# One half-head's loads moved ahead of the finished half-head's last sums, and the softmax maximum formed negated, in a hybrid attention block

## The chip, the cores and the metric

The kernel runs on one core of a Trainium2 chip. The metric is device time in microseconds (us) of the whole kernel, the median of several runs. The engines are TensorE (PE in the profile, its weight loads PEld), VectorE (DVE), ScalarE (ACT), GpSimd (POOL) and SyncE (SP, which issues every DMA of this kernel).

## What is computed

One decoder layer on a sequence of 2048 tokens with 1024 channels, in float32: token mixing, then a SwiGLU feed-forward part, then a norm. The change touches token mixing, which has two attention branches.

- Branch A: twelve heads of 64 channels in three groups. Group g attends with dilation 1, 4 or 16 inside a band of 129 keys, with a linear (ALiBi) bias. The outputs of the three groups are merged with weights from their softmax denominators.
- Branch B: four heads of "forgetting attention", causal over the whole sequence:

```python
s = einsum('bqhd,bkhd->bhqk', qi, k) * scale
s = s + (Fi[..., :, None] - F[..., None, :])
s = where(kpos[None, :] <= qpos[:, None], s, -inf)
out = einsum('bhqk,bkhd->bqhd', softmax(s), v)
```

Each branch goes through an up-projection, is gated and summed, and one output projection follows.

## The kernel before

**Program order and issue order.** The kernel is traced in program order. At build time a planner then lays out one fixed queue of instructions for each engine. It takes instructions as their operands and their tile slots become ready on its own timeline, earlier program order first. So a load may stand in SP's queue far ahead of its place in the program, if a slot for its tile is free. On the chip each queue runs in order, and semaphores hold an instruction until its operands are there.

**Tile slots.** On-chip buffers are slots that tiles of one tag share (`SLOTS`, L77). Three tags matter here. `big` has 11 slots of 8 KB per partition: the queries, keys and key remainders of a branch A head take three, those of a branch B half-head two or four, and each up-projection pass takes four for its tiles `y` (L993). `mid` has 6 slots of 4 KB: branch A's values `va` and the rows `nf` of branch B. `bigx` has 3 slots, for `utok` and the merge tiles `uw`.

**Branch A** (`branch_a`, `head_a`). For each of 12 heads and four quarters u, `scores` makes four blocks of 128 queries by 128 or 256 keys: two matmuls into PSUM (L769, L773), one DVE instruction that adds the bias, writes the logits to SBUF and takes the row maximum (L775), then one small DVE instruction that negates the four maxima (L778), and four exponentials on ACT (L783). `sums` transposes the exponentials on PE, copies them out and multiplies them with the values.

**Branch B** (`branch_b`, `head_f`, `half_tiles`). Heads 0 and 1 are done whole; heads 2 and 3 are done as halves of the queries, in the order

```python
FOX = ((None, 0), (None, 1), (0, 2), (0, 3), (1, 2), (1, 3))
```

where the first number is the half (0: queries 0 to 1023, 1: queries 1024 to 2047) and the second the head. I write half-head (1, 2) for the second half of head 2. `head_f` starts by asking for its data: `half_tiles` issues the loads of queries `qs` (L710), keys `kh` and `kl` (L712) and values `vhl` (L713), and L840 the rows `nf`. `scores(cq, b)` works on 128 queries against all keys up to them, in segments of 512: POOL makes the bias (L854, L859), PE two matmuls (L866), DVE adds, writes logits and carries the maximum from segment to segment (L868); then DVE negates the maximum (L874), ACT takes the exponentials and their sums `dp` (L878), and DVE adds the segments' sums up (L880). `sums(cq)` follows one step later: transposes (L902), a split into two float32r parts (L106, L107), and matmuls with the values (L910), for 256 queries; every second time it writes the result out (L922), and that counts in `f_done`.

**The order around the change.** Two generators run side by side by a clock of costs written by hand, first branch A and B, later the up-projection `up(0)` and B:

```python
together([(ga, PACE[0]), (gb, 1.0)])
merge_weights()
together([(gb, 1.0)], lambda: f_done[0] >= 12)
gu = up(0)
together([(gu, PACE[1]), (gb, 1.0)])
for g in (gb, gu, up(1)): ...
```

Branch A ends while half-head (0, 3) is in its last score passes. `merge_weights` (L973 to L988) works out branch A's merge weights and stores them (`wrow`). B then runs until (0, 3) is written out, which is the twelfth time. Only then is `up(0)` traced, and `half_tiles` for (1, 2) after the first step of `up(0)`. The first four steps of `up(cp)` load branch outputs and weights for half of the tokens (L999, L1005), multiply and add them on DVE (L1007, L1009) and split the result into the `y` tiles; sixteen more steps each multiply with up-projection weights (L100 to L102 into psZ), apply two gates on DVE (L1034), add on POOL (L1035) and store. Ten of the sixteen steps of `up(0)` stand among the score passes of the last two half-heads.

Of the kernel before, what the change touches and what calls it, by code (L numbers as in the profile page):

```python
# [10 lines left out]
F32 = mybir.dt.float32  # L11
# [48 lines left out]
def trunk(ctx, tc, x, c, w_ada, b_ada, norm_mix, w_in, b_forget, w_up_a, w_up_b, w_out,  # L60
# [63 lines left out]
    cst.tile([P, 16], F32, name="fill")  # L124
# [620 lines left out]
    def head_a(h):  # L745
# [5 lines left out]
        mx = sm.tile([P, NT], F32, tag="mxa", name="mxa")  # L751
# [3 lines left out]
        def scores(u):  # L755
# [4 lines left out]
            for b in range(4):  # L760
                if b % 2 == 0:
                    s = psS("A")
                bb = 4 * u + b
                so = s[:, (b % 2) * 256:(b % 2) * 256 + 256]
                k0 = bb * P if first[b] else (bb - 1) * P
                o0 = P if first[b] else 0
                for i, kk in enumerate((kh, kl)):
                    if g == 2:
                        PE.matmul(so[:, o0:].rearrange("p (c n) -> p c n", c=NCH), qs[:, bb * P:(bb + 1) * P],  # L769
                                  kk.rearrange("p (c r n) -> p r c n", c=NCH, r=16)[:, bb],  # L770
                                  start=(i == 0), stop=(i == 1))
                    else:
                        PE.matmul(so[:, o0:], qs[:, bb * P:(bb + 1) * P], kk[:, k0:(bb + 1) * P],  # L773
                                  start=(i == 0), stop=(i == 1))
                V.tensor_tensor_reduce(out=Lb(b, o0, 256), in0=so[:, o0:], in1=bias[:, o0:],  # L775
                                       scale=1.0, scalar=NEG, op0=ALU.add, op1=ALU.max,
                                       accum_out=mx[:, bb:bb + 1])
            V.tensor_scalar(nm[:, 4 * u:4 * u + 4], mx[:, 4 * u:4 * u + 4], -1.0, None,  # L778
                            op0=ALU.mult)
            for b in range(4):  # L780
                bb = 4 * u + b
                o0 = P if first[b] else 0
                A.activation(Lb(b, o0, 256), Lb(b, o0, 256), AF.Exp, bias=nm[:, bb:bb + 1])  # L783
            return Lb, first

        def sums(u, Lb, first):
# [42 lines left out]
            PE.transpose(pst[:NT, :P], mx, ident)  # L829
# [5 lines left out]
    def head_f(h, part):  # L835
# [7 lines left out]
        def scores(cq, b):  # L843
            if cq % 2 == 0 and b == 0:
                den[cq // 2] = sm.tile([P, 4], F32, tag="den", name="den", bufs=4)
            qb = 2 * cq + b
            nk = (qb + 1) * P
            dq = den[cq // 2][:, qb % 4:qb % 4 + 1]
            mx = sm.tile([P, 4], F32, tag="mx", name="mx", bufs=4)
            segs = list(range(0, nk, CH))  # L850
            for i, sg in enumerate(segs):
# [13 lines left out]
                for j, kk in enumerate((kh, kl)):  # L865
# [4 lines left out]
                    scale=1.0, scalar=NEG if i == 0 else mx[:, i - 1:i],  # L870
                    op0=ALU.add, op1=ALU.max, accum_out=mx[:, i:i + 1])
            n = len(segs)
            nm = sm.tile([P, 1], F32, tag="nmf", name="nmf", bufs=4)
            V.tensor_scalar(nm, mx[:, n - 1:n], -1.0, None, op0=ALU.mult)  # L874
            dp = sm.tile([P, 4], F32, tag="dp", name="dp", bufs=4)
            for i, sg in enumerate(segs):
                e = min(sg + CH, nk)
                A.activation(Ls[cq, b, sg][:, :e - sg], Ls[cq, b, sg][:, :e - sg], AF.Exp, bias=nm,  # L878
                             accum_out=dp[:, i:i + 1])
            V.tensor_reduce(out=dq, in_=dp[:, :n], op=ALU.add, axis=mybir.AxisListType.X)  # L880

        def sums(cq):
            if cq % 2:
                dn = den[cq // 2]
# [43 lines left out]
    def branch_b():  # L928
# [3 lines left out]
        for part, h in FOX:  # L932
            scores, sums = head_f(h, part)
# [7 lines left out]
            if (part, h) in (FOX[-1], FOX[-3]):  # L941
                yield from behind()
                behind = None
# [20 lines left out]
    def merge_weights():  # L964
# [9 lines left out]
        for g in (1, 2):  # L974
            V.tensor_tensor(v3(M, g), v3(M, g), tok(g), op=ALU.max)
        for g in range(3):
            V.tensor_tensor(v3(es[g], g), tok(g), v3(M, g), op=ALU.subtract)
# [257 lines left out]
```

## Time and profile before

| | |
|---|---|
| Three runs | 2929.98 us median, 2927.61 to 2929.99 |
| The profiled execution | 2929.82 us, of which 2927.8 us are the span from first to last instruction |
| Busy share of the span | PE 95%, DVE 70%, ACT 47%, POOL 6% |
| Mean granted TensorE clock | 0.983 of full speed |

The busy share is a mean over stages. The attention stage lies between about 840 and 1455 us from the start; before it are the input projections, after it the output projection and the feed-forward part. PE's busy time is modelled, and matmuls are pipelined, so a PE that is 97% busy may still have small gaps.

### The profile page before, as it was taken

Reading aid. Unit: us, or ns where it says so; the run is one execution under the profiler, and the core shown is the slowest. Engines: PE = TensorE matmul, PEld = TensorE weight load, DVE = VectorE, ACT = ScalarE, POOL = GpSimd, SP = SyncE. Lnnn points to the kernel's source line nnn. Section 1 sums busy time; section 2 is a strip of 40 time slices with the busy share of each in tenths; the row PEclk is TensorE's granted clock in tenths of the full one; section 3 lists DMA queues with packets and bytes.
Section 4 is the critical chain, followed back from the end, with each engine's and each line's share of the span. In section 5 each row is a group of like instructions: output and inputs, shape, how many; then the busy total and the mean of one; then the engine's idle time right before and its main releaser. Section 6 shows DMA issues by size and latency. Waiting matters only on the chain.

```text
span 2927.8 us, 40828 instructions
## 1 busy us (share of the span) xinstructions
PE 2776.7 (95%) x13778; PEld 2310.3 (79%) x13778; DVE 2050.0 (70%) x4283; ACT 1376.6 (47%) x2726; POOL 182.2 (6%) x291
## 2 busy tenths in 40 slices
PE   7999999999999999478799999999999999989998
PEld 6789888988888888367577788888888888878876
DVE  5865578576647888676877866656855557796887
ACT  4653345344447778444355633334433335343543
POOL 0000000000002223242300000000000000000000
PEclk9999999999999999789999999999999999999999
DMA  7687476467856767766956654443522235785642
GB/s 245 167 222 216 130 218 196 152 172 204 249 190 229 239 179 205 231 193 197 324 174 211 200 174 144 144 158 116 176 78 85 87 113 161 219 259 178 214 156 99
DMA packets 524089, 534.70 MB, mean 183 GB/s; under 512 B 91716, under 2 KB 374748, under 8 KB 517724
## 3 DMA queue, kind: packets, MB, share of 16 engines
q1 hardware_dynamic: 523880, 532.11, 58.4%
q8 instruction: 108, 1.77, 0.2%
q14 instruction: 101, 0.83, 0.1%
HBM read 360.70 MB, written 171.29 MB: 182 GB/s over the span
## 4 chain that ended last, share of the span: by engine, by line
PE 45%; DVE 2%; DMA 2%; issue 1%; ACT 1%; POOLq 0%; DVEq 0%; SPq 0%; ACTq 0%
PE psX L100 9%; PE psX L101 9%; PE psX L102 8%; PE psZ L100 4%; PE psZ L101 4%; PE psZ L102 4%; PE psY L102 2%; PE psY L100 2%; PE psY L101 2%; DMA pc<-wfg 1%; PE psT L1110 0%; DVE wl L107 0%; DMA out_dram<-x 0%; ACT wh L106 0%; DVE wt L217 0%
## 5 line engine op out<-in xcount | busy, mean ns | idle before, releaser
L106 ACT ACTIVATE wh<-wt 128x512 fp32r<-128x512 f32 (+1 forms) x464 | 288.5, 623 | 628.1 <-PE psX L101 338.6
L107 DVE TENSOR_TENSOR wl<-wt,wh 128x512 fp32r<-128x512 f32 (+1 forms) x464 | 313.6, 679 | 258.8 <-ACT wh L106 241.6
L106 ACT ACTIVATE wh<-wr 128x512 fp32r<-128x512 f32 (+1 forms) x324 | 201.5, 623 | 428.2 <-PE psX L101 233.5
L107 DVE TENSOR_TENSOR wl<-wr,wh 128x512 fp32r<-128x512 f32 (+1 forms) x324 | 219.4, 678 | 201.4 <-ACT wh L106 184.5
L217 DVE TENSOR_TENSOR wt<-wr 128x512 f32<-128x512 f32 (+1 forms) x216 | 147.2, 681 | 11.6 <-DMA wr<-in_w_in_dram 4.8
L217 DVE TENSOR_TENSOR wt<-wr,wt 128x512 f32<-128x512 f32 (+1 forms) x216 | 146.5, 678 | 3.7
L244 ACT ACTIVATE u<-psX 128x512 f32<-128x512 f32 x216 | 125.6, 582 | 8.7 <-PE psX L102 8.7
L854 POOL TENSOR_SCALAR bi<-nf,F_col 128x512 f32<-128x512 f32 (+3 forms) x160 | 107.1, 670 | 303.1 <-DVE mx L868 258.7
L878 ACT ACTIVATE L<-L,nmf 128x512 f32<-128x512 f32 (+3 forms) x160 | 103.1, 647 | 36.0 <-DVE nmf L874 35.9
L106 ACT ACTIVATE ph<-psT 128x512 fp32r<-128x512 f32 (+1 forms) x110 | 61.3, 566 | 71.5 <-PE psT L902 71.0
L1140 DVE TENSOR_TENSOR ac<-psZ,u 128x512 f32<-128x512 f32 x88 | 60.3, 685 | 41.4 <-PE psZ L102 40.2
L107 DVE TENSOR_TENSOR pl<-psT,ph 128x512 fp32r<-128x512 f32 (+1 forms) x110 | 70.5, 646 | 20.6 <-ACT ph L106 20.2
L811 PE MATMUL psY<-pf,va 128*65 128x128 f32 (+1 forms) x408 | 78.8, 327 | 0.8 <-DVE den L880 0.2
L775 DVE CUSTOM_DVE_ANT_0 L<-psX,bias 128x128 f32<-128x128 f32 (+1 forms) x192 | 64.1, 356 | 18.8 <-PE psX L773 14.1
L910 PE MATMUL psY<-pl,vhl 128*128 128x256 f32 x248 | 70.4, 311 | 6.6 <-DVE pl L107 5.7
L910 PE MATMUL psY<-ph,vhl 128*128 128x256 f32 (+1 forms) x248 | 72.0, 302 | 4.4 <-ACT ph L106 3.2
L783 ACT ACTIVATE L<-L,nm 128x128 f32<-128x128 f32 (+1 forms) x192 | 72.2, 450 | 5.5 <-DVE nm L778 4.7
L100 PE MATMUL psZ<-y,wu 128*128 128x512 f32 x128 | 54.4, 425 | 17.9 <-DVE gt L1034 13.9
L100 PE MATMUL psX<-f_A11h,wh 128*128 128x512 f32 x176 | 69.4, 394 | 0.0
L902 PE MATMUL psT<-ident,L 128*128 128x128 f32 x410 | 67.6, 285 | 1.8 <-DVE pl L107 1.8
L101 PE MATMUL psX<-f_A11l,wh 128*128 128x512 f32 x176 | 69.0, 392 | 0.0
L102 PE MATMUL psX<-f_A11h,wl 128*128 128x512 f32 x176 | 69.0, 392 | 0.0
(542 smaller groups left out, 8701.2 us busy)
## 6 DMA issues: line engine op xcount, KB each, us to landing
x<-x SPq DMA_DIRECT2D x192, 256.0 KB
wr<-in_w_ffn_in_dram SPq DMA_DIRECT2D x88, 512.0 KB
wr<-in_w_in_dram SPq DMA_DIRECT2D x64, 512.0 KB
qk<-sh SPq DMA_DIRECT2D x192, 128.0 KB
act<-ac SPq DMA_DIRECT2D x88, 256.0 KB
pc<-wfg SPq DMA_DIRECT2D x77, 256.0 KB
qk<-st SPq DMA_DIRECT2D x128, 128.0 KB
wa<-in_w_ada_dram SPq DMA_DIRECT2D x64, 256.0 KB
```

The source lines that it names most:

```text
L100: PE.matmul(o, lh, rh, start=first, stop=False, skip_group_check=True)
L101: PE.matmul(o, lh, rl, start=False, stop=False, skip_group_check=True)
L102: PE.matmul(o, ll, rh, start=False, stop=last, skip_group_check=True)
L106: A.activation(hi, src, AF.Copy)
L107: V.tensor_tensor(lo, src, raw(hi), op=ALU.subtract)
L217: V.tensor_tensor(v[i], *made[i](g, v), op=ALU.subtract)
L244: A.activation(t, o, AF.Copy, scale=1.0 if scale is None else scale)
L783: A.activation(Lb(b, o0, 256), Lb(b, o0, 256), AF.Exp, bias=nm[:, bb:bb + 1])
L811: PE.matmul(uo[:65, qb_[0] * P:qb_[0] * P + w], va[:, 4 * u + kb_, :], pf[:, pos:pos + w], start=i_ == 0, stop=i_ == len(runs) - 1, skip_g ...
L854: G.tensor_scalar(bi[:, :e - sg], nf[sg // D][:, sg % D:sg % D + e - sg], 1.0, F_col[:, qb * NHB + h:qb * NHB + h + 1], op0=ALU.mult, op1= ...
L878: A.activation(Ls[cq, b, sg][:, :e - sg], Ls[cq, b, sg][:, :e - sg], AF.Exp, bias=nm, accum_out=dp[:, i:i + 1])
L910: f_pe[0] = PE.matmul(uo[:, q0:256], vhl[:, kb, :], p_[:, 256 * i:256 * i + 256 - q0], start=(kp == 0 and i == 0 and j == 0), stop=(last a ...
```

## The change

Three things. First, after the last score pass of (0, 3) the next half-head's `head_f(2, 1)`, with all of its loads, is traced ahead of the last `sums` of (0, 3), of its write-out and of the first step of `up(0)`. The same line does nothing at the end of (1, 3), which is the last. The rest of the program order is as it was. Second, the score instructions of both branches scale by -1 and take a minimum, so that they leave the negated logits and the negated maximum; the two small negating instructions go, and the exponential takes scale -1. The branch A merge reads the negated maxima, with `max` turned into `min` and the two operands of a subtraction swapped. Third, the sums `dp` of four score passes are kept in one tile and added up by one DVE instruction in `sums`, once for 512 queries. A filler tile grows by 16 columns, which belongs to no instruction.

```diff
--- before.py
+++ after.py
@@ -121,7 +121,7 @@
         return r
 
 
-    cst.tile([P, 16], F32, name="fill")
+    cst.tile([P, 32], F32, name="fill")
     ident = cst.tile([P, P], F32, name="ident")
     make_identity(nc, ident)
     ones = cst.tile([P, P], F32, name="ones")
@@ -748,7 +748,6 @@
         qs, kh, kl, va = head_tiles(h // 2, 6 + h // 2, h % 2, g, sl, d)
         bias = slot("pc", "bias", [P, 256])
         G.tensor_scalar(bias, base, float(slopes[h] * d), 0.0, op0=ALU.mult, op1=ALU.add)
-        mx = sm.tile([P, NT], F32, tag="mxa", name="mxa")
         nm = sm.tile([P, NT], F32, tag="nm", name="nm")
         ut = slot("bigx", "utok", [65, T])
 
@@ -773,14 +772,12 @@
                         PE.matmul(so[:, o0:], qs[:, bb * P:(bb + 1) * P], kk[:, k0:(bb + 1) * P],
                                   start=(i == 0), stop=(i == 1))
                 V.tensor_tensor_reduce(out=Lb(b, o0, 256), in0=so[:, o0:], in1=bias[:, o0:],
-                                       scale=1.0, scalar=NEG, op0=ALU.add, op1=ALU.max,
-                                       accum_out=mx[:, bb:bb + 1])
-            V.tensor_scalar(nm[:, 4 * u:4 * u + 4], mx[:, 4 * u:4 * u + 4], -1.0, None,
-                            op0=ALU.mult)
+                                       scale=-1.0, scalar=-NEG, op0=ALU.add, op1=ALU.min,
+                                       accum_out=nm[:, bb:bb + 1])
             for b in range(4):
                 bb = 4 * u + b
                 o0 = P if first[b] else 0
-                A.activation(Lb(b, o0, 256), Lb(b, o0, 256), AF.Exp, bias=nm[:, bb:bb + 1])
+                A.activation(Lb(b, o0, 256), Lb(b, o0, 256), AF.Exp, bias=nm[:, bb:bb + 1], scale=-1.0)
             return Lb, first
 
         def sums(u, Lb, first):
@@ -826,7 +823,7 @@
             SP.dma_start(u_scr[h // 2][(h % 2) * 64:(h % 2) * 64 + 64, :], ut[:64, :])
             SP.dma_start(den_scr[h].rearrange("(a t) -> a t", a=1), ut[64:65, :])
             pst = ps("Y")
-            PE.transpose(pst[:NT, :P], mx, ident)
+            PE.transpose(pst[:NT, :P], nm, ident)
             str_ = slot("pc", "str", [NT, P])
             V.tensor_copy(str_, pst[:NT, :P])
             SP.dma_start(sta_scr[h], str_)
@@ -842,11 +839,12 @@
 
         def scores(cq, b):
             if cq % 2 == 0 and b == 0:
-                den[cq // 2] = sm.tile([P, 4], F32, tag="den", name="den", bufs=4)
+                den[cq // 2] = [sm.tile([P, 4, cq // 2 + 1], F32, tag=f"dp{cq // 2}", name="dp"),
+                                sm.tile([P, 4], F32, tag="den", name="den")]
             qb = 2 * cq + b
             nk = (qb + 1) * P
-            dq = den[cq // 2][:, qb % 4:qb % 4 + 1]
-            mx = sm.tile([P, 4], F32, tag="mx", name="mx", bufs=4)
+            dp = den[cq // 2][0][:, qb % 4, :]
+            nm = sm.tile([P, 4], F32, tag="nmf", name="nmf", bufs=4)
             segs = list(range(0, nk, CH))
             for i, sg in enumerate(segs):
                 e = min(sg + CH, nk)
@@ -867,21 +865,18 @@
                               start=(j == 0), stop=(j == 1))
                 V.tensor_tensor_reduce(
                     out=L[:, :e - sg], in0=s[:, :e - sg], in1=bi[:, :e - sg],
-                    scale=1.0, scalar=NEG if i == 0 else mx[:, i - 1:i],
-                    op0=ALU.add, op1=ALU.max, accum_out=mx[:, i:i + 1])
+                    scale=-1.0, scalar=-NEG if i == 0 else nm[:, i - 1:i],
+                    op0=ALU.add, op1=ALU.min, accum_out=nm[:, i:i + 1])
             n = len(segs)
-            nm = sm.tile([P, 1], F32, tag="nmf", name="nmf", bufs=4)
-            V.tensor_scalar(nm, mx[:, n - 1:n], -1.0, None, op0=ALU.mult)
-            dp = sm.tile([P, 4], F32, tag="dp", name="dp", bufs=4)
             for i, sg in enumerate(segs):
                 e = min(sg + CH, nk)
-                A.activation(Ls[cq, b, sg][:, :e - sg], Ls[cq, b, sg][:, :e - sg], AF.Exp, bias=nm,
-                             accum_out=dp[:, i:i + 1])
-            V.tensor_reduce(out=dq, in_=dp[:, :n], op=ALU.add, axis=mybir.AxisListType.X)
+                A.activation(Ls[cq, b, sg][:, :e - sg], Ls[cq, b, sg][:, :e - sg], AF.Exp,
+                             bias=nm[:, n - 1:n], scale=-1.0, accum_out=dp[:, i:i + 1])
 
         def sums(cq):
             if cq % 2:
-                dn = den[cq // 2]
+                dp, dn = den[cq // 2]
+                V.tensor_reduce(out=dn, in_=dp, op=ALU.add, axis=mybir.AxisListType.X)
                 V.reciprocal(dn, dn)
                 pd = ps("Y")
                 PE.transpose(pd[:4, :P], dn, ident)
@@ -929,8 +924,10 @@
 
 
         behind = None
-        for part, h in FOX:
-            scores, sums = head_f(h, part)
+        nxt = None
+        for at_, (part, h) in enumerate(FOX):
+            scores, sums = nxt or head_f(h, part)
+            nxt = None
             for cq in range(4 if part else 0, 4 if part == 0 else 8):
                 for b in range(2):
                     scores(cq, b)
@@ -939,6 +936,9 @@
                         yield from behind()
                 behind = lambda sums=sums, cq=cq: sums(cq)
             if (part, h) in (FOX[-1], FOX[-3]):
+                if at_ + 1 < len(FOX):
+
+                    nxt = head_f(FOX[at_ + 1][1], FOX[at_ + 1][0])
                 yield from behind()
                 behind = None
     f_end, f_done, f_pe = [None], [0], [None]
@@ -972,9 +972,9 @@
         M, Dn, *es = [mw[:, i, :] for i in range(5)]
         V.tensor_copy(M, md[0][:, 0, 0, :])
         for g in (1, 2):
-            V.tensor_tensor(v3(M, g), v3(M, g), tok(g), op=ALU.max)
+            V.tensor_tensor(v3(M, g), v3(M, g), tok(g), op=ALU.min)
         for g in range(3):
-            V.tensor_tensor(v3(es[g], g), tok(g), v3(M, g), op=ALU.subtract)
+            V.tensor_tensor(v3(es[g], g), v3(M, g), tok(g), op=ALU.subtract)
             A.activation(es[g], es[g], AF.Exp)
         for g in range(3):
             if g == 0:
```

## Rows read from the trace of the kernel before

**Rows 1.** The page: busy time by engine, and PE's busy tenths in 40 slices.

```profile
PE 2776.7 (95%) x13778; PEld 2310.3 (79%) x13778; DVE 2050.0 (70%) x4283; ACT 1376.6 (47%) x2726; POOL 182.2 (6%) x291
...
PE   7999999999999999478799999999999999989998
```

**Rows 2.** Busy time by stretch: stretch, its length, then busy us (and instructions).

```profile
core 0: us, PE busy (x) PEld busy (x) DVE busy (x) ACT busy (x) POOL busy (x), PEclk, DMA share, GB/s
880.00:1187.50 307.50, 293.57 (x2063) 254.18 (x2062) 249.37 (x977) 239.98 (x577) 83.08 (x168) 0.99 0.67 205
960.00:1000.00 40.00, 39.28 (x286) 34.32 (x284) 33.45 (x115) 28.00 (x69) 9.27 (x21) 1.00 0.71 232
1150.00:1160.00 10.00, 9.82 (x82) 9.18 (x81) 8.62 (x45) 9.93 (x29) 3.93 (x8) 1.00 0.10 21
1187.50:1216.50 29.00, 0.28 (x3) 0.14 (x2) 12.67 (x17) 1.53 (x3) 0.00 (x0) 0.58 0.79 226
1206.00:1216.50 10.50, 0.00 (x0) 0.00 (x0) 3.71 (x4) 0.00 (x0) 0.00 (x0) 0.50 1.03 325
1216.50:1376.00 159.50, 130.24 (x682) 106.49 (x683) 119.40 (x271) 79.28 (x190) 61.23 (x80) 0.88 0.68 207
```

**Rows 3.** The timeline of PE around its hole: start, duration, instruction, [idle before].

```profile
1173.76 0.28 PE L769 MATMUL psX<-kl,qs 128*128 128x128 f32 x1
...
1187.50 0.28 PE L910 MATMUL psY<-pl,qv 128*128 128x128 f32 x1
...
1216.52 1.22 PE L866 MATMUL psX<-kh,qs 128*128 128x512 f32 x2 [28.74 <-DMA kh<-qk]
```

**Rows 4.** Waits of PE, 1216 to 1360 us: total, times, longest.

```profile
PE psX L866 <- DMA kh<-qk: 28.7, 1, 28.7
...
PE psX L866 <- DMA kl<-qk: 1.2, 1, 1.2
```

**Rows 5.** The timeline of SP's queue, 1140 to 1280 us.

```profile
1143.39 0.54 SPq L840 DMA_DIRECT2D nf<-nf  x1
...
1180.10 0.32 SPq L832 DMA_DIRECT2D sta<-str  x1
...
1190.37 1.54 SPq L988 DMA_DIRECT2D wrow<-mw  x3
...
1205.94 0.52 SPq L710 DMA_DIRECT2D qs<-qk  x1
1206.55 0.38 SPq L712 DMA_DIRECT2D kh<-qk  x1
```

**Rows 6.** The timeline of ACT: the first write to a `y` tile.

```profile
1204.08 1.15 ACT L106 ACTIVATE y<-uw 128x512 fp32r<-128x512 f32 x2 [15.88 <-DVE uw L1009]
```

**Rows 7.** DMA issues, 1140 to 1280 us: count and KB each.

```profile
kh<-qk SPq DMA_DIRECT2D x2, 1024.0 KB
```

**Rows 8.** DVE by shape, 830 to 1380 us: count | busy us, mean ns | idle before.

```profile
L868 DVE CUSTOM_DVE_ANT_0 L<-psZ,bi 128x512 f32<-128x512 f32 x36 | 24.5, 681 | 3.9 <-PE psZ L866 3.5 <-PE psT L800 0.2
...
L868 DVE CUSTOM_DVE_ANT_0 L<-psX,bi,mx 128x512 f32<-128x512 f32 x29 | 21.5, 742 | 2.9 <-issue 1.1 <-PE psX L866 0.6 <-PE psT L902 0.5
...
L874 DVE TENSOR_SCALAR nmf<-mx 128x1 f32<-128x1 f32 x64 | 9.3, 145 | 0.5
L778 DVE TENSOR_SCALAR nm<-mxa 128x4 f32<-128x4 f32 x48 | 8.0, 167 | 0.2
```

**Rows 9.** Instructions on tile `dp`: ns min/median/max, then DVE's idle time before them.

```profile
L880 DVE TENSOR_REDUCE den<-dp x64: 121/150/157, 884.3 to 1357.6; 128x1 f32<-128x1 f32 x16, 128x1 f32<-128x2 f32 x16, 128x1 f32<-128x3 f32 x16, 128x1 f32<-128x4 f32 x16
...
  ACT L L878: 9.3, 11
```

**Rows 10.** Line 244 on ACT, whole span: ns min/median/max.

```profile
L244 ACT ACTIVATE u<-psX x216: 572/581/601, 94.3 to 2911.9; 128x512 f32<-128x512 f32 x108
```

**Rows 11.** POOL's gate sums: line 1035, 1185 to 1500 us, and the eleventh of 32.

```profile
L1035 POOL TENSOR_TENSOR gt<-gt x32: 1268/1296/4014, 1269.0 to 1455.1; 128x512 f32<-128x512 f32 x32
...
1368.45 1.30 POOL L1035 TENSOR_TENSOR gt<-gt 128x512 f32<-128x512 f32 x1 [22.47 <-DVE gt L1034]
```

## The prediction

> **What bounds the kernel now.** I read the page first: PE is busy 95% of the span, and its 40 slices show where it isn't, the first slice and the four from 1171 us on [rows 1]. The rest is nearly all nines, so a change to this kernel can win much only in that hole and in the stage around it. Then the busy times by stretch [rows 2]. From 880 to 1187.5 us, branch A beside branch B, PE is busy 293.6 of 307.5 us, and DVE, at 84% in the stretch from 960 to 1000 us, comes next. From 1187.5 to 1216.5 us PE does nothing at all, while DVE is busy 12.7 of 29 us. From 1216.5 to 1376 us (the last two half-heads beside the first part of the up-projection) PE is busy 82%, DVE 75%, and no engine is full.
>
> Third, what ended the hole. PE's last matmul of half-head (0, 3) starts at 1187.50 us, and the next one, the first score of (1, 2), at 1216.52 us, 28.74 us later, held by the load of `kh` [rows 3]. The load of `kl` then costs another 1.2 us [rows 4]. So the hole is 29.9 us, and one late group of loads makes it.
>
> Fourth, why the loads were late. On SP's queue `qs` and `kh` were issued at 1205.94 and 1206.55 us [rows 5], and the transfer took up to the hole's end. The `nf` rows of the same half-head, traced later in the same function, were issued as early as 1143.39 us [rows 5]. They use another tag, so what kept the keys back was their slots. Traced ahead of them on the tag `big` are the four `y` tiles of the up-projection; the first write to a `y` is ACT's at 1204.08 us [rows 6], and `qs` goes out 1.9 us behind it. The first write had to wait for merge weights and broadcasts. I read this as slots given out in program order: the loads stood behind four tiles that were not yet wanted.
>
> **The moved loads.** The change traces all of (1, 2)'s loads (`qs`, `kh`, `kl`, `vhl`, two `nf`) ahead of the `y` tiles. What holds them then is only free slots. Of 11, the dilated heads 10 and 11 hold three each and the half-heads (0, 2) and (0, 3) two each, so one is free, and head 10's three come free when head 11 has taken over. At the latest, head 11's last score at 1173.76 us [rows 3] frees three more. Taking the old 13 us from the issue of `qs` to the arrival of `kl` (1205.94 us to 1216.52 + 1.2 + 1.2 us), the keys are there by 1187 us even in that late case, when PE runs dry; in the likely case they go out near 1150 us. `kh` is 1024 KB [rows 7], `kl` and `vhl` are of the same size and `qs` loads half of the tokens: 3584 KB or 3.67 MB, or 11.3 us at the 325 GB/s of the end of the hole [rows 2]. The new place has room: at 1150 to 1160 us the transfers have a DMA share of 0.10, and in the old place 1.03 [rows 2]. The two `nf` are out before 1150 us already and don't move.
>
> On SP's queue the loads now pass the stores of (0, 3)'s result and of the merge weights (`wrow` at 1190.37 us) and all loads of the up-projection. If the planner places one before its slot is free on the chip, the queue stands still, and behind it are branch A's last statistics (from 1180.10 us) [rows 5] and so the merge. Between 1173.76 and 1180.10 us there are 6.3 us of slack; if the last tile instead waits for (0, 3)'s last matmul at 1187.50 us, the merge comes up to 7.4 us later, but scores don't need it. I take nothing, and keep 7.4 us as the bound of a loss. The Trainium skill, "DMA: Bandwidth & Descriptors", section "Anatomy of one DMA", states the rule that speaks against moving loads up: DMA engines don't wait on semaphores, any wait is held by the issuing queue ahead of dispatch. By it the sum would be 7.4 us higher if a slot came late, by the slack it stays as it is.
>
> What the hole was good for must be done elsewhere: DVE's 12.7 us of merge work. So I bound the gain of this stage by DVE. From 1187.5 to 1376 us it does 12.7 + 119.4 = 132.1 us. The change takes 16 score passes x (145 + 148 ns) = 4.7 us out of it and adds 4 x 0.15 us, so 128.0 us. At the 75% of 1216.5 to 1376 us that takes 171 us and ends at 1358 us, 17.5 us earlier. At the 84% of 960 to 1000 us it takes 152 us, and 36 us are won. The mean of the two, 27 us, lies just under the hole's 29.9 us; I take 27. The granted clock was 0.58 in the hole and 0.88 after it [rows 2]; PE doesn't set the pace there, so I add nothing for it.
>
> **The negated maximum.** 48 instructions on `nm` at 167 ns and 64 on `nmf` at 145 ns [rows 8] go, and 64 additions of `dp` at 150 ns [rows 9] become 16, which I cost at the same 0.15 us. That is 8.0 + 9.3 + 9.6 - 2.4 = 24.5 us off DVE, and with it the 9.3 us in which DVE stood still until ACT had its sums [rows 9]; the new addition comes a step later, when they are long there. By the shares of instructions 48, 48 and 48 - 12 lie before 1187.5 us: 8.0 + 7.0 + 7.2 - 1.8 = 20.4 us. What of it reaches PE? From 880 to 1187.5 us PE has 307.5 - 293.6 = 13.9 us idle for all reasons [rows 2], so the gain lies between 0 and 13.9 us. I take 3 us, near the lower end, since PE is 95% busy.
>
> The score instruction itself: 160 + 192 of them, add-and-maximum at 681 ns for 128x512 [rows 8], become add-and-minimum with scale -1. The trace doesn't show that form. The low bound is no change; for the high bound I take the nearest dearer form, with one column operand more, at 742 ns [rows 8]: 352 x 0.061 us = 21.5 us of DVE, which would eat up most of what was taken off. I take 0, since the streams and the columns stay as they are. The exponential's scale -1: line 244 copies with scale 0.125 for queries and 1.0 otherwise, and all 216 lie between 572 and 601 ns [rows 10], so a scale costs nothing that shows. Each exponential now waits for its own maximum, not for four; bound 0 to a gain already inside the 13.9 us. The merge's swapped operations and the filler cost nothing, since their count and sizes stay.
>
> **The sum.** 2929.8 us (the profiled execution: 2927.8 us of span and 2.0 us around it, 0.2 us under the median of the runs) - 27 - 3 = 2900 us. What follows 1376 us is taken to move up as a block.
>
> **Rivals.** (a) *DVE sets the pace from 880 to 1187.5 us too.* PE's busy time is modelled, so small gaps may hide in it; then all 20.4 us come off instead of 3: 2929.8 - 27 - 20.4 = 2882 us. For it: DVE at 84%. Against: 13.9 us of PE idle in all. The Trainium skill, "Trainium Kernel Development and Optimization", section "Performance Expectations", states the rule behind it, that matmul busy time is a bad measure of how near TensorE is to its limit because matmuls are pipelined; no row here settles by how much.
>
> (b) *The up-projection sets the end.* Its merge chain starts at the same time as before, and if the steps behind it, not the half-heads, are the longer row, only the loads' 11.3 us of DMA time come out of its way: 2929.8 - 11.3 - 3 = 2916 us. For it: its 22 last sums run alone after the half-heads, from 1368.45 us on [rows 11]. Against: ten of 32 run among the scores without holding them.
>
> (c) *The loads stay late.* The planner leaves them behind the merge's loads on SP; the hole remains and only DVE's work shrinks: 3 + 2 us, 2925 us.
>
> (d) *Scores crowd out the up-projection (slower).* The half-heads now take DVE, SBUF slots and PSUM in the time of the merge; up-projection steps that ran among the scores fall behind them, where a step takes (1455.1 - 1368.45) / 21 = 4.1 us [rows 11]. If all ten are pushed out, 41 us are lost against 30 won: 2941 us. It decides from 30 / 4.1 = 7.3 steps on. Against: in those steps nothing waits for the scores' result, and the loads they need find a freer DMA.
>
> **Chances.** The forecast 0.67 (its own range 2929.8 - 36 - 13.9 = 2880 to 2929.8 - 17.5 = 2912 us); (a) 0.08; (b) 0.12; (c) 0.07; (d) 0.06. The range that leaves out no more than 2 in 10 is 2880 to 2920 us: it holds nearly all of the forecast, most of (a) and (b), and leaves out (c) and (d). A difference under 0.2% (5.9 us) is about what a measurement of this kernel can't tell from no change. Faster by more: the forecast, (a), (b), 0.87; within it: (c), 0.07; slower: (d), 0.06.
>
> **What would show it.** In the new profile: the loads of (1, 2) on SP's queue before 1180 us; no wait of PE on `kh` over 2 us; PE over 60% busy from 1187 to 1216 us and a granted clock over 0.9 there; the last half-head's result stored near 1350 us; the first sum of the up-projection before 1260 us, and ten of them, give or take two, before the scores end; no instructions at `nm` and `nmf`, 16 additions of `dp`, DVE's busy total near 2025 us; the score instruction still at 0.68 us for 512 columns. I am wrong if the loads wait for slots until `y` is written, if a dearer score instruction fills DVE again, or if the time won at 1216 us is lost again before 1455 us.

## The result

The changed kernel takes 2893.55 us (median of four runs, 2890.47 to 2895.48) against 2929.23 us before (median of four, 2927.61 to 2929.99): a ratio of 0.988, with a 95% interval of 0.9861 to 0.9895, or 36 us. The forecast was 2900 us, in a range of 2880 to 2920 us. The profiled execution took 2890.47 us, 2888.6 us of it span, 39.2 us less than the span before.

The page of the changed kernel, busy time by engine and PE's busy tenths in 40 slices:

```profile
PE 2772.3 (96%) x13778; PEld 2309.1 (80%) x13778; DVE 2039.4 (71%) x4123; ACT 1383.0 (48%) x2730; POOL 189.0 (7%) x291
...
PE   7999999999999999887899999999999999999998
```

The digits 4787 behind 1171 us [rows 1] have become 8878. PE's busy total hardly moves: what went is idle time. The stretches of the changed kernel, with the columns of [rows 2]:

```profile
880.00:1187.50 307.50, 296.19 (x2095) 259.27 (x2093) 243.49 (x861) 247.75 (x592) 89.08 (x179) 0.98 0.71 219
...
1187.50:1216.50 29.00, 22.92 (x120) 17.54 (x121) 26.54 (x64) 19.03 (x48) 12.11 (x18) 0.88 0.66 198
1206.00:1216.50 10.50, 7.81 (x32) 6.40 (x33) 10.08 (x19) 4.46 (x10) 3.51 (x3) 0.67 1.07 368
1216.50:1340.00 123.50, 102.80 (x545) 82.38 (x543) 99.08 (x185) 58.41 (x136) 48.62 (x51) 0.94 0.84 247
```

In the 29 us in which PE did 0.28 us of work before, it does 22.9, and DVE 26.5 instead of 12.7. SP's queue of the changed kernel shows why (start, time on the queue, instruction):

```profile
1138.02 0.92 SPq L710 DMA_DIRECT2D qs<-qk  x1
...
1149.48 0.34 SPq L712 DMA_DIRECT2D kh<-qk  x1
...
1150.39 0.44 SPq L712 DMA_DIRECT2D kl<-qk  x1
1150.92 0.60 SPq L713 DMA_DIRECT2D vhl<-v  x1
...
1178.91 0.67 SPq L829 DMA_DIRECT2D sta<-str  x1
...
1196.41 1.29 SPq L988 DMA_DIRECT2D wrow<-mw  x3
```

`kh` goes out at 1149.48 us instead of 1206.55 us [rows 5]. PE's timeline of the changed kernel then has the first score of (1, 2) ahead of the last matmul of (0, 3), not 29 us behind it [rows 3]:

```profile
1173.32 0.40 PE L864 MATMUL psX<-kh,qs 128*128 128x512 f32 x1
...
1186.53 0.28 PE L905 MATMUL psY<-pl,qv 128*128 128x128 f32 x1
```

And among PE's waits of the changed kernel from 1150 to 1345 us (total, times, longest) there is none on `kh` or `kl` any more, where [rows 4] had 28.7 and 1.2 us:

```profile
PE psY L905 <- DVE pl L107: 15.5, 13, 3.6
PE psX L864 <- DVE nmf L866: 6.0, 11, 1.2
```

The table follows the gain through the stages, in us from the span's start; it is read from the first and last instruction of each group in the profiled executions of six kernels (the last four are experiments, below).

| | last matmul of (0, 3) | first score of (1, 2) | last score | last value matmul | last gate sum | span |
|---|---|---|---|---|---|---|
| before | 1187.5 | 1216.5 | 1349.0 | 1375.5 | 1455.1 | 2927.8 |
| after | 1186.5 | 1173.3 | 1309.3 | 1337.3 | 1421.0 | 2888.6 |
| loads alone | 1195.3 | 1178.6 | 1319.7 | 1349.5 | 1431.4 | 2902.7 |
| negated maximum and one sum alone | 1182.1 | 1209.9 | 1331.9 | 1356.4 | 1435.5 | 2905.7 |
| hop back in branch A | 1190.8 | 1177.2 | 1316.9 | 1345.5 | 1431.6 | 2902.7 |
| copies back beside the chains | 1183.9 | 1170.5 | 1310.3 | 1336.6 | 1416.6 | 2889.3 |

By the last gate sum 34.1 us are won. The other 5.1 us come behind it: 1472.7 us from there to the end before, 1467.6 us after, and 1467.7 to 1477.3 us in the experiments, where that part of the program has the same work in each. So a step of a few us between two profiles isn't to be put down to one edit.

### The profile page after: what moved, and what is told of

The parts are those of the page before. It is cut to its first block, busy times and chain, and to the rows that moved or that the text cites. A ratio compares the mean times of both kernels' runs of the same rounds, so it can differ in the third digit from the quotient of the medians.

```text
span 2888.6 us, 40722 instructions
## 1 busy us (share of the span) xinstructions
PE 2772.3 (96%) x13778; PEld 2309.1 (80%) x13778; DVE 2039.4 (71%) x4123; ACT 1383.0 (48%) x2730; POOL 189.0 (7%) x291
## 4 chain that ended last, share of the span: by engine, by line
PE 49%; DMA 5%; DVE 4%; ACT 2%; issue 1%; SPq 0%; POOLq 0%; DVEq 0%; POOL 0%; ACTq 0%
PE psX L100 9%; PE psX L101 9%; PE psX L102 9%; PE psZ L100 5%; PE psZ L101 4%; PE psZ L102 4%; PE psY L100 2%; PE psY L101 2%; PE psY L102 2%; DMA uw<-wrow 1%; PE psY L905 1%; DMA gt<-g 1%; DMA uw<-u 1%; DMA uw<-rc 0%; DMA m<-gt 0%
## 5 line engine op out<-in xcount | busy, mean ns | idle before, releaser
L873 ACT ACTIVATE L<-L,nmf 128x512 f32<-128x512 f32 (+3 forms) x160 | 103.3, 648 | 15.8 <-DVE nmf L866 15.5
L780 ACT ACTIVATE L<-L,nm 128x128 f32<-128x128 f32 (+1 forms) x192 | 78.8, 453 | 12.4 <-DVE nm L774 11.7
L107 DVE TENSOR_TENSOR pl<-psT,ph 128x512 fp32r<-128x512 f32 (+1 forms) x110 | 70.6, 646 | 12.6 <-ACT ph L106 12.5
L905 PEld LDWEIGHTS psY<-pl,vhl 128*128 128x128 f32 x248 | 50.0, 202 | 25.0 <-DVE pl L107 23.1
L100 PE MATMUL psZ<-f_S4h,wh 128*128 128x512 f32 x176 | 68.7, 390 | 0.2 <-DVE ac L1140 0.2
```

What stands on the lines that cost most here:

```text
L100: PE.matmul(o, lh, rh, start=first, stop=False, skip_group_check=True)
L107: V.tensor_tensor(lo, src, raw(hi), op=ALU.subtract)
L905: f_pe[0] = PE.matmul(uo[:, q0:256], vhl[:, kb, :], p_[:, 256 * i:256 * i + 256 - q0], start=(kp == 0 and i == 0 and j == 0), stop=(last a ...
```

## Experiments

Each was timed in turn with the kernel before, whose medians were 2929.3, 2929.9 and 2930.2 us in the three groups. Intervals are 95%.

**Loads alone.** The kernel before with only the new `nxt` lines of `branch_b`.

```diff
+        nxt = None
+        for at_, (part, h) in enumerate(FOX):
+            scores, sums = nxt or head_f(h, part)
...
+                    nxt = head_f(FOX[at_ + 1][1], FOX[at_ + 1][0])
```

> The kernel before with the moved loads alone; score instructions and sums as before. Theory (the moved loads are nearly the whole gain, since they let the scores of (1, 2) start about 43 us sooner, and DVE is only the next limit): 2895 to 2902 us, PE's wait for kh gone, first score of (1, 2) near 1175 us. Rival (a good part of the gain is DVE work and waits taken out by the negated maximum): 2905 to 2915 us.

Measured: 2904.86 us, ratio 0.9921 (0.9908 to 0.9935), 24.5 us under before and between the two ranges that were expected. `kh` goes out at 1155.9 us and the hole is gone. The loads carry most of the gain, but 11.3 us of it are missing.

**Negated maximum and one sum alone.** The changed kernel with the old `branch_b`.

> The changed kernel without the moved loads: negated maximum and one sum of dp for four passes, program order of the loads as before. Theory: the hole of 29 us stays and the time is 2922 to 2929 us; the 20 us of DVE work taken out ahead of 1187 us bring 0 to 3 us there, because PE sets the pace. Rival (DVE sets the pace from 880 to 1187 us): 2905 to 2915 us, with the hole beginning at about 1170 us.

Measured: 2909.76 us, ratio 0.9937 (0.9924 to 0.9951), 19.6 us under before. That is the rival's time and not the theory's, but the rival's sign is missing: the hole begins at 1182.1 us, not near 1170. It is still there, as PE's waits of this kernel from 1150 to 1345 us show:

```profile
PE psX L864 <- DMA kh<-qk: 27.4, 1, 27.4
```

The table shows where its gain comes from: 5.4 us by the end of (0, 3), and the two half-heads behind the hole, from first score to last value matmul, take 146.5 us instead of 159.0. The two parts alone sum to 44.1 us and together give 36: they overlap by 8 us.

**What held the loads.** Three kernels ask by what order slots of the tag `big` are handed out. The first names the four `y` tiles ahead of the loads and writes them where they were written:

```diff
+                    y0.append([[slot("big", "y", [P, 4, CH], F32R) for _ in "hl"] for _ in range(2)])
                     nxt = head_f(FOX[at_ + 1][1], FOX[at_ + 1][0])
...
-        y = [[slot("big", "y", [P, 4, CH], F32R) for _ in "hl"] for _ in range(2)]
+        y = y0.pop() if y0 else [[slot("big", "y", [P, 4, CH], F32R) for _ in "hl"] for _ in range(2)]
```

> The changed kernel, but the four y tiles of the first up-projection pass are named in the program just ahead of the moved loads; their first write stays where it was. Theory (slots of a tag are given out in the order in which the program names the tiles, so the loads waited behind y): the loads go out again behind the first write to y, near 1205 us, the hole is back and the time is 2920 to 2928 us. Rival (the loads were late because they stood behind the up-projection's loads on SP, or slots go by the first write): no difference from the changed kernel, 2890 to 2897 us.

Measured: 2892.69 us, ratio 0.9873 (0.9859 to 0.9886), as the change. `kh` went out at 1145.96 us. The order in which tiles are named does nothing.

The second traces the loads behind the write-out and sums of (0, 3), but still ahead of the up-projection's first step:

```diff
-                    nxt = head_f(FOX[at_ + 1][1], FOX[at_ + 1][0])
-                yield from behind()
+                for step in behind():
+                    if f_done[0] == 12 and nxt is None and at_ + 1 < len(FOX):
+                        nxt = head_f(FOX[at_ + 1][1], FOX[at_ + 1][0])
+                    yield step
```

> The changed kernel, but the loads of (1, 2) are traced behind the last sums and the write-out of (0, 3), and still ahead of the up-projection's first step. Theory (only the place ahead of the y tiles matters): as the changed kernel, 2889 to 2899 us, loads issued before 1160 us. Rival (the loads must pass the write-out and the merge on SP's queue): loads behind 1189 us, 10 us or more of the hole stay, 2903 to 2915 us.

Measured: 2893.26 us, ratio 0.9877 (0.9863 to 0.9890), again as the change. The write-out is not what the loads had to be moved past.

The third traces them inside the up-projection's first step, after its loads and multiplications and just ahead of the first write to a `y`:

```diff
-            scores, sums = nxt or head_f(h, part)
-            nxt = None
+            scores, sums = early.pop() if early else head_f(h, part)
...
-                    nxt = head_f(FOX[at_ + 1][1], FOX[at_ + 1][0])
...
+            if cp == 0 and p_ == 0:
+                early.append(head_f(FOX[4][1], FOX[4][0]))
             for c_ in range(2):
                 split(y[c_][0][:, p_, :], y[c_][1][:, p_, :], acc[:, c_ * CH:(c_ + 1) * CH])
```

> The changed kernel, but the loads of (1, 2) are traced inside the up-projection's first step, behind its loads and multiplications and just ahead of its first write to the y tiles. Theory (a slot of the tag goes by the order of the first writes; the loads stood behind y's): loads near 1150 us and the time of the changed kernel, 2890 to 2896 us. Rival (the loads stood behind the up-projection's loads and broadcasts on SP's queue): loads near 1200 us, the hole is back, 2905 to 2912 us as with the negation alone.

Measured: 2892.92 us, ratio 0.9872 (0.9855 to 0.9888). SP's queue of this kernel, with the loads out as early as in the change:

```profile
1137.61 0.90 SPq L710 DMA_DIRECT2D qs<-qk  x1
...
1146.81 0.34 SPq L712 DMA_DIRECT2D kh<-qk  x1
```

On the chip its first `y` is written at 1211.21 us, 64 us later. With the old place, in the kernel with the negated maximum alone, ACT's timeline and SP's queue show the loads again right behind that write:

```profile
1198.02 1.15 ACT L106 ACTIVATE y<-uw 128x512 fp32r<-128x512 f32 x2 [15.13 <-DVE uw L1004]
```

```profile
1199.87 0.52 SPq L710 DMA_DIRECT2D qs<-qk  x1
1200.49 0.38 SPq L712 DMA_DIRECT2D kh<-qk  x1
```

So slots of this tag go by the order of first writes in the program. A load traced behind the first write to `y` gets its slot only when that write has been made.

**Which edit brings the 11 us.** Two kernels take one of the small edits back at a time. With the loads and the one addition of `dp`, but maximum and negation as before:

```diff
-                                       scale=-1.0, scalar=-NEG, op0=ALU.add, op1=ALU.min,
-                                       accum_out=nm[:, bb:bb + 1])
+                                       scale=1.0, scalar=NEG, op0=ALU.add, op1=ALU.max,
+                                       accum_out=mx[:, bb:bb + 1])
+            V.tensor_scalar(nm[:, 4 * u:4 * u + 4], mx[:, 4 * u:4 * u + 4], -1.0, None,
+                            op0=ALU.mult)
...
```

> The moved loads and the one sum of dp for four passes, with the maximum and its negation as before. The moved loads alone gave 2904.9 us and the whole change 2893.6 us, so 11 us are to be shared out. Theory (in the loop, DVE's queue stood still for ACT's sums, and behind it the scores and POOL's bias): the one sum brings 6 us or more of the 11, so 2894 to 2899 us. Rival (the negation between maximum and exponential was the dear part): 2901 to 2905 us.

Measured: 2898.31 us, ratio 0.9889 (0.9874 to 0.9904). With the loads and the negated maximum, but an addition of `dp` in each pass:

```diff
+            V.tensor_reduce(out=dq, in_=dp[:, :n], op=ALU.add, axis=mybir.AxisListType.X)
```

> The moved loads and the negated maximum, with a sum of dp in every score pass as before. Theory (the wait of DVE for ACT's sums is the dear part): 2899 to 2904 us. Rival (the negation step is the dear part): 2894 to 2898 us.

Measured: 2895.58 us, ratio 0.9880 (0.9866 to 0.9895). Taken back one at a time, the edits cost 4.8 and 2.0 us; taken back together 11.3. The first time is the one expected if the one sum were the dear part, the second the one expected if the negation were. No interval parts either of the two from the change, so these two runs alone don't say where the 11 us are.

**DVE's busy time or its place in the chain.** Two kernels change how much DVE does and leave its chains alone. The first adds small copies that nobody waits for, one for each group of passes in branch A and one or two for each in branch B:

```diff
+    def idle4(src):
+        V.tensor_scalar(sm.tile([P, 4], F32, tag="scr", name="scr")[:, :src.shape[1]], src, 1.0, None, op0=ALU.mult)
...
+            idle4(nm[:, 4 * u:4 * u + 4])
...
+            idle4(nm[:, n - 1:n])
+            if qb % 4:
+                idle4(nm[:, n - 1:n])
```

> The changed kernel with 160 small DVE instructions put back at the same places, each copying a maximum into a scratch tile that nobody reads: DVE has the busy time of before the negation, and no chain and no wait for ACT has it. Theory A (DVE's busy time sets the pace of the two last half-heads and partly before): back to 2901 to 2906 us. Theory B (what counted was the chain from maximum to exponential and the wait for ACT): 2893 to 2897 us.

Measured: 2890.52 us, ratio 0.9864 (0.9850 to 0.9879): no slower than the change. DVE's busy time (third column behind the length) was put back, by the stretch from 880 to 1340 us, first the changed kernel, then this one:

```profile
880.00:1340.00 460.00, 421.90 (x2757) 359.18 (x2755) 369.12 (x1108) 325.20 (x773) 149.81 (x248) 0.97 0.74 226
```

```profile
880.00:1340.00 460.00, 416.67 (x2754) 353.55 (x2752) 379.54 (x1266) 325.02 (x772) 147.91 (x248) 0.97 0.75 225
```

The second moves the merge's eight additions of 1.2 us each from DVE to POOL:

```diff
-                    V.tensor_tensor(uu, uu, acc, op=ALU.add)
+                    G.tensor_tensor(uu, uu, acc, op=ALU.add)
```

> The changed kernel with the eight additions of the merge tiles (128x1024, 1.22 us each on DVE) on POOL: 9.7 us of work taken off DVE in the stage of the two last half-heads. Theory (a chain sets the pace there, not DVE's busy time): no gain, 2891 to 2899 us, rather a loss where POOL's biases stand behind the additions. Rival (DVE's busy time sets the pace, as the prediction's bounds had it): 2882 to 2887 us.

Measured: 2892.89 us, ratio 0.9869 (0.9855 to 0.9884): no gain, with DVE at 363.4 us in the same stretch instead of 369.1. DVE 10.4 us busier or 5.7 us less busy, the time is the same.

Then the hop alone: a DVE copy between maximum and exponential, where the negation had stood, in branch A only,

```diff
+            V.tensor_scalar(n2[:, 4 * u:4 * u + 4], nm[:, 4 * u:4 * u + 4], 1.0, None, op0=ALU.mult)
...
-                A.activation(Lb(b, o0, 256), Lb(b, o0, 256), AF.Exp, bias=nm[:, bb:bb + 1], scale=-1.0)
+                A.activation(Lb(b, o0, 256), Lb(b, o0, 256), AF.Exp, bias=n2[:, bb:bb + 1], scale=-1.0)
```

> The changed kernel with one small DVE copy put between the four maxima of branch A and its exponentials, where the negation stood; branch B as changed. Theory (the chain from maximum to exponential costs, and it costs in the stretch where both branches run): most of the 5 us that separate the changed kernel (2893.6) from the one with negations in both branches (2898.3), so 2896 to 2899 us. Rival (branch A's chain is hidden; the cost lies in branch B): 2890 to 2895 us.

Measured: 2904.99 us, ratio 0.9912 (0.9897 to 0.9926), 11.4 us over the change, level with the loads alone and over both ranges that were expected. In branch B only:

```diff
+            n2 = sm.tile([P, 1], F32, tag="n2", name="n2", bufs=4)
+            V.tensor_scalar(n2, nm[:, n - 1:n], 1.0, None, op0=ALU.mult)
...
-                             bias=nm[:, n - 1:n], scale=-1.0, accum_out=dp[:, i:i + 1])
+                             bias=n2, scale=-1.0, accum_out=dp[:, i:i + 1])
```

> The changed kernel with one small DVE copy put between the last maximum of a score pass of branch B and its exponentials; branch A as changed. Theory (the chain counts most where branch B's two last half-heads run beside the up-projection): 2896 to 2899 us. Rival (it is branch A's chain, or neither alone): 2890 to 2895 us.

Measured: 2892.85 us, ratio 0.9873 (0.9858 to 0.9887): nothing. Of the hop in A, the stretch from 880 to 1170 us shows a part in PE's busy time (first column behind the length), first the changed kernel, then the one with the hop in A:

```profile
880.00:1170.00 290.00, 279.64 (x1982) 245.39 (x1981) 228.89 (x816) 233.00 (x554) 80.97 (x165) 0.98 0.73 228
```

```profile
880.00:1170.00 290.00, 274.71 (x1943) 236.86 (x1942) 228.90 (x843) 227.61 (x541) 80.02 (x163) 1.00 0.72 223
```

DVE is busy for the same 228.9 us in both, and PE 4.9 us less with the hop. By the table 3.9 us are lost by the first score and 10.6 by the last gate sum, so the greater part is lost after branch A has ended.

Branch A itself ends later in every kernel with such a hop. These are A's exponentials (192 each, ns min/median/max, first and last start) in the changed kernel, with the hop in A, and with the loads and one sum, where the negation is such a hop:

```profile
L780 ACT ACTIVATE L<-L,nm x192: 355/492/530, 878.2 to 1172.0; 128x256 f32<-128x256 f32 x108, 128x128 f32<-128x128 f32 x84
```

```profile
L782 ACT ACTIVATE L<-L,n x192: 357/492/515, 890.3 to 1176.8; 128x256 f32<-128x256 f32 x108, 128x128 f32<-128x128 f32 x84
```

```profile
L783 ACT ACTIVATE L<-L,nm x192: 358/493/529, 889.2 to 1177.1; 128x256 f32<-128x256 f32 x108, 128x128 f32<-128x128 f32 x84
```

The last exponential starts at 1176.8 to 1179.7 us in the four kernels with a hop in A (these two, the kernel before and the loads alone), and at 1168.5 to 1172.5 us in the ten without one. The total doesn't follow as evenly: the same delay of 5 us goes with a loss of 11.4 us in one kernel and 4.8 us in the other, and their runs don't overlap (2904.49 to 2905.23 against 2896.00 to 2900.46 us).

The hop does two things. It adds an instruction, and it makes the four exponentials of a quarter wait for the fourth maximum, as ACT's timelines show at A's start, first the changed kernel, then the one with the hop in A:

```profile
878.19 0.40 ACT L780 ACTIVATE L<-L,nm 128x128 f32<-128x128 f32 x1
...
882.54 0.51 ACT L780 ACTIVATE L<-L,nm 128x256 f32<-128x256 f32 x1
```

```profile
890.28 1.60 ACT L782 ACTIVATE L<-L,n 128x128 f32<-128x128 f32 x4
```

In branch B the exponentials of a pass wait for its last maximum with or without the hop. That may be why it costs nothing there; no run parts the wait from the instruction.

**The next wait.** In the changed kernel ACT waits for the up-projection's weights, for 18.7 us in the stretch below (the expectation has 31 us). A version asks for the weights of step j + 1 ahead of step j:

```diff
-        for j in range(KT):
+        def w_load(j):
...
+            return r
+        ahead = w_load(0)
+        for j in range(KT):
+            r, ahead = ahead, w_load(j + 1) if j + 1 < KT else None
```

> The changed kernel with the up-projection's weights of step j + 1 asked for ahead of step j. In the changed kernel ACT stands 31 us behind these weights from 1165 to 1340 us, and the splits of the exponentials are queued behind. Theory (that wait is on the path of the sums): 2885 to 2891 us. Rival (the time is set elsewhere, or the loads only take DMA time from others): 2891 to 2898 us.

Measured: 2889.35 us, ratio 0.9859 (0.9843 to 0.9876), the lowest median here, 4.2 us under the change by the medians, but the intervals overlap. ACT's waits from 1165 to 1340 us, first the changed kernel, then this one, show the wait halved:

```profile
ACT wu L106 <- DMA wr<-in_w_up_b_dram: 18.7, 5, 7.4
```

```profile
ACT wu L106 <- DMA wr<-in_w_up_b_dram: 9.0, 5, 3.8
```

## Why the prediction was right, and where it was not

**The late loads.** "The loads stood behind four tiles that were not yet wanted" held, and "program order" means the order of first writes; the order of naming fell with its experiment. "In the likely case they go out near 1150 us" was right to a microsecond. What it costs the queue was small too: SP stood 3.3 us before `kh`, and branch A's last statistics left at 1178.91 us, 1.2 us sooner than before, so the bound of 7.4 us wasn't needed. With the loads alone they left 5.0 us later, at 1185.11 us. The merge weights `wrow` left 6.0 us later, after a wait of 7.0 us for DVE; the first gate sum came 8.8 us sooner all the same.

That the time fitted so closely is in part luck. The prediction counted on the slots of head 10; `kh` got one of the half-head (0, 2), behind its last score, which ended at 1149.45 us. SP's wait and that score of the changed kernel:

```profile
SPq L712 <- PE psZ L864: 3.3, 1, 3.3
```

```profile
1148.82 0.63 PE L864 MATMUL psZ<-kk,qv 128*128 128x512 f32 x2
```

**The stage: 27 us.** The loads alone brought 24.5 us. Nothing of the negation is in that, while the 27 us counted 4.7 us of DVE's work as gone; without it the same working gives 176.1 us at 75% and 157.3 us at 84%, so 12.4 to 31.2 us and a mean of 21.8. The size is right, but the reason isn't, so the size is luck: I bounded the stage by DVE's share, and it came out at (26.5 + 99.1) / 152.5 = 82% from 1187.5 to 1340 us, inside the two bounds, but more or less work on DVE moved nothing. What sets the pace there instead is not settled. PE's largest waits in total, 15.5 us in 13 times, are on `pl`, the end of the chain from score over DVE, ACT and PE's transposes back to DVE, which fits a chain better than a full engine; that is an argument, not a run.

**The negated maximum: 3 us.** This is the term that was mis-sized. It is 11.3 us on top of the loads (2904.86 - 2893.55) and 19.6 us by itself. The step that failed: "I take 3 us, near the lower end, since PE is 95% busy". It looked only at PE's idle time before 1187.5 us, and there the size was near: with the old loads, half-head (0, 3) ended 5.4 us sooner. But the last two half-heads and the up-projection gained too, as the runs of each part alone show. And the saving was booked as 24.5 us of DVE time, which the copies show to be worth nothing where they stand in no chain.

What cost time, in part at least, was a DVE instruction between branch A's four maxima and their exponentials: it ends A some 5 us later, and the whole kernel 4.8 us later in one experiment (with the negations of branch B besides) and 11.4 us in the other. In branch B 64 of them cost nothing. "Each exponential now waits for its own maximum, not for four" was the place to look, and the prediction gave it nothing. Open stays how 5 us become 11.4: 48 hops at 167 ns [rows 8] are 8.0 us in all, and the greater part of that loss fell after A's end. Each edit also changes the order in which instructions are laid out on all engines; the wait, the instruction and the order were not told apart.

**Costed at nothing.** The add-and-minimum score instruction, by DVE's shapes in the changed kernel from 830 to 1340 us:

```profile
L866 DVE CUSTOM_DVE_ANT_0 L<-psZ,bi 128x512 f32<-128x512 f32 x36 | 24.5, 683 | 3.3 <-PE psZ L864 2.9
...
L866 DVE CUSTOM_DVE_ANT_0 L<-psX,bi,nmf 128x512 f32<-128x512 f32 x29 | 21.5, 740 | 2.0 <-POOL bi L852 0.8 <-PE psX L864 0.7 <-DVE nmf L866 0.3
```

683 and 740 ns against 681 and 742 [rows 8]: the bound of 21.5 us fell away. The additions of `dp`, by the view of the tile:

```profile
L879 DVE TENSOR_REDUCE den<-dp x16: 108/156/170, 899.6 to 1318.6; 128x4 f32<-128x4 f32 x4, 128x4 f32<-128x8 f32 x4, 128x4 f32<-128x12 f32 x4, 128x4 f32<-128x16 f32 x4
...
  ACT L L873: 5.9, 5
```

Sixteen at 156 ns, as costed; but DVE still waits 5.9 us there for ACT, against 9.3 [rows 9]. "They are long there" was wrong for the sum of a group's last pass.

**The rivals.** (a), DVE as the pace before 1187.5 us too, fell with the copies. (b) didn't happen: the last gate sum moved up by 34.1 us with the half-heads. (c) fell with SP's queue. (d) neither: nine gate sums start ahead of the last score at 1309.3 us and the tenth at 1310.56 us, just behind it, where ten ran among the scores before, and the eleventh comes at 1330.49 us instead of 1368.45 [rows 11]:

```profile
1310.56 1.58 POOL L1035 TENSOR_TENSOR gt<-gt 128x512 f32<-128x512 f32 x1 [5.12 <-ACT ph L106]
1330.49 1.28 POOL L1035 TENSOR_TENSOR gt<-gt 128x512 f32<-128x512 f32 x1 [18.34 <-DVE gt L1034]
```

**Signs that were foretold.** The last result's store left at 1341.2 us (near 1350), the first gate sum at 1260.2 (before 1260, so by a hair not), PE was 79% busy in the old hole (over 60%). Two missed: the granted clock there was 0.88, not over 0.9, and DVE's total fell by 10.6 us, not 24.5, though exactly the 160 instructions went. Their lengths make 24.3 us. Other instructions of DVE took 9.3 us more, half of it beside POOL (below); the other 4.4 us are overlaps of successive instructions, which busy time counts only once.

## What to carry to other kernels

Where a load is issued late, ask which tile holds its slot and when that tile is first written; here it was enough to trace the load ahead of that write, and three places ahead of it gave the same time. A busy share tells where to look, not what sets the pace: put the same work back beside the chain, and then in the chain, before an edit's gain is booked as engine time. Price a small instruction by the chain that it stands in: 48 of them between branch A's maxima and exponentials went with 5 to 11 us, depending on what else was changed, and 160 beside the chains with none. And give an edit no single price while another stands beside it: the negated maximum and the one sum gave 20 us alone and 11 us on top of the loads.

## What the hardware showed unexpectedly

**DVE beside POOL.** Some of DVE's instructions take over twice as long as others of their shape, and the traces show what ran at the same time. One of the longest of the changed kernel with the POOL sum beside it, then such a pair of the kernel before:

```profile
1379.74 1.78 DVE L183 TENSOR_TENSOR pc<-pc 128x512 f32<-128x512 f32 x1
...
1379.37 1.61 POOL L1035 TENSOR_TENSOR gt<-gt 128x512 f32<-128x512 f32 x1 [1.89 <-DVE gt L1034]
```

```profile
1429.47 1.78 DVE L181 TENSOR_TENSOR s<-s,pc 128x512 f32<-128x512 f32 x1
...
1429.03 1.68 POOL L1035 TENSOR_TENSOR gt<-gt 128x512 f32<-128x512 f32 x1 [1.23 <-DVE gt L1034]
```

Among DVE's instructions whose shape has a median of 0.6 us or more, 10 took over 1.3 times that median in the kernel before, and 17 in the changed kernel. Every one of them overlaps an instruction of POOL, nearly always a gate sum (10 and 15). Among the two-operand instructions of that size that read no PSUM and ran beside no POOL instruction, over 1800 in each trace, none took more than 1.04 times its median (0.68 us at 128x512); those that read PSUM beside a gate sum (62 and 49) took at most 1.03 times. The excess of the long ones is 7.7 us before and 12.5 us after. Which lines they belong to differs from kernel to kernel, so the mean of a few instructions can move without the change having touched them: the four at line 181 went from 1136 to 679 ns, the four at line 183 from 682 to 1207 ns.

**The clock.** The mean of 0.67 from 1206 to 1216.5 us hides two levels. Finer stretches of the changed kernel (TensorE's granted clock is the third number from the end):

```profile
1196.00:1203.00 7.00, 6.39 (x38) 4.58 (x37) 5.63 (x19) 6.55 (x17) 4.01 (x8) 1.00 0.63 152
1203.00:1209.00 6.00, 1.91 (x10) 1.28 (x10) 4.99 (x7) 2.45 (x7) 0.70 (x1) 0.97 1.06 303
1209.00:1215.00 6.00, 5.57 (x22) 4.74 (x23) 6.00 (x11) 2.14 (x5) 2.42 (x2) 0.50 1.05 375
1216.00:1221.00 5.00, 4.15 (x25) 3.01 (x23) 3.90 (x9) 4.39 (x11) 2.58 (x3) 1.00 1.05 246
```

In the 6 us up to 1209 us PE was busy for 1.91 us, nearly all of it at full speed (2.4 GHz). Then the clock was at the lower level (1.2 GHz) for 6 us, while PE was busy for 5.57 us, and from 1216 us at full speed again. In the kernel before, where PE stood still, the clock was 0.50, the lower level, from 1206 to 1216.5 us [rows 2].
